# Seven products for the gate and up projections of two feed-forwards, with two weight sums made by accumulating transfers

## The chip, the cores and the metric

The kernel runs on one core of one Trainium2 chip. The metric is the device time of one execution in microseconds. TensorE multiplies, VectorE (DVE) and ScalarE (ACT) do the elementwise work, GpSimd (POOL) issues some transfers and clears a few tiles, and SyncE (SP) issues most transfers.

## The reference

One inference step of a two-layer decoder trunk, for a prompt of 512 tokens with 16 meta tokens and for 8 sample tokens (536 columns in all), width 1024, in float32. Each layer is a feed-forward, a mixer and a second feed-forward:

```python
def swiglu(h, w_gu, w_down):
    gate, up = jnp.split(h @ w_gu, 2, axis=-1)      # w_gu: 1024 x 5632
    return (jax.nn.silu(gate) * up) @ w_down         # w_down: 2816 x 1024
x += 0.5 * swiglu(rmsnorm(x, g), ...); x += mix(rmsnorm(x, g)); x += 0.5 * swiglu(rmsnorm(x, g), ...)
```

The mixer of layer 0 is convolution beside windowed attention; that of layer 1 is a state-space scan (SSM), whose output passes through a gated linear unit (GLU).

## The kernel before

Activations stand transposed: eight residual tiles `x[d]` of 128 rows (width) by 536 columns (tokens), in two halves of 268. float32 products are made from exact high and low parts: weights `whi`, `wlo` and activations `xh`, `xl`. `gemm` (L130) makes, for each 128-row slice `k` of the contraction and each half, three matmuls of 268 columns: `whi*xh`, `whi*xl`, `wlo*xh`. A 128x1024 weight block thus costs 8 x 3 x 2 = 48 matmuls.

`weights` (L117) loads such a block on SP's queue into `raw` (4 buffers), ACT rounds it to `whi` (L126, 3 buffers) and DVE subtracts to get `wlo` (L127, 3 buffers).

`ffn` (L255) goes in three chunks of 8, 8 and 6 hidden tiles. Of each hidden tile it makes a gate product and an up product (a pair of blocks, 96 matmuls), scales both by the norm's factor `R` (L273, L275), takes the silu (L274), multiplies (L276) and splits the result into `mh`, `ml` (`put`, L143, with ACT at L146 and DVE at L147). Then come the chunk's eight down products, added to the residual (L288). In the last chunk `finalize` (L149) scales and splits each finished residual tile into `xh`, `xl` (L155, L156) and sums its squares (L162, L163) for the next stage's norm, whose factor `rstd` (L179) computes.

`ssm_prep` (L758) is a generator of 45 steps that builds the matrices of layer 1's recurrence on DVE and stores them with 59 transfers on POOL's queue. It is advanced once per gate/up pair and once per down product (`filler`) through the second feed-forward of layer 0 and the first of layer 1, some 34 calls in each. `_mixer1` (L935) then runs the recurrence and ends with the GLU.

The program is written in one order; a scheduler orders each engine's queue ahead of the run by its own model of times and gives out buffers in turn. At run time each engine works its queue in order, waiting on semaphores. Accumulators are three pairs of PSUM banks (`mm` twice, `S` once, L95 to L103) and two single banks `ms`.

Of the kernel before, what the change touches and what calls it, by code (L numbers as in the profile page):

```python
# [26 lines left out]
NCK = 66            # chunks of 8 tokens in the prompt  # L27
# [3 lines left out]
LOENG = lambda nc: nc.vector  # L31
WHOLE, HEAD = 3, tuple((d,) for d in range(8))
# [28 lines left out]
class Trunk:  # L61
# [4 lines left out]
    # ---------------------------------------------------------------- pools  # L66
# [45 lines left out]
    # ------------------------------------------------------- building blocks  # L112
# [30 lines left out]
    def put(self, hi, lo, src):  # L143
        """src (fp32) -> exact high and low parts."""
# [4 lines left out]
    def finalize(self, d, g):  # L149
        """residual tile d is complete: its scaled split parts and its squares."""  # L150
# [3 lines left out]
        if g < 6:  # L154
# [99 lines left out]
    # ---------------------------------------------------------- feed-forward  # L254
    def ffn(self, wgu, wdn, gnext, filler=None, fin=None, head=None):  # L255
# [3 lines left out]
        for f0, nf in ((0, 8), (8, 8), (16, 6)):  # L259
            for i in range(nf):  # L260
# [20 lines left out]
            if f0 == 16 and fin is not None:  # L281
                self.down_last(fin, dn, nf)
                return
            for d in range(ND):
# [6 lines left out]
                if filler is not None and d < 6:  # L291
# [62 lines left out]
        # the samples' convolution up to the new row  # L354
# [19 lines left out]
        # states that are moved, not computed  # L374
# [7 lines left out]
    def mixer0(self, p, gnext):  # L382
# [12 lines left out]
        # gated conv input  # L395
# [3 lines left out]
        def z_tile(c):  # L399
# [7 lines left out]
            # sigmoid(g) = (1 + tanh(g / 2)) / 2: the table set that holds exp, too  # L407
# [19 lines left out]
        def conv_pe(i):  # L427
            """eight taps of the last tile's convolution, as products with diagonal matrices"""
# [18 lines left out]
        # keys, values, queries  # L447
# [858 lines left out]
```

## Time and profile before

| | |
|---|---|
| runs shown, us | 2070.46, 2066.05, 2066.57; median 2066.57 |
| span of the profiled execution | 2071.1 us (the page gives no other time of it) |
| busy: TensorE, DVE, ACT, POOL | 98%, 55%, 31%, 6% of the span |
| matmuls | 16302 |
| mean granted clock of TensorE | 0.989 of full speed |
| bytes moved by transfers | 213.51 MB, mean 103 GB/s |

Busy times are sums of the intervals in which an engine had an instruction running. A TensorE that is busy all the time may still be running its pipeline at its normal pace, so the distance between starts of matmuls is the measure of its work. The span is what the profiler saw between the first and the last instruction.

### The profile page before, as it was taken

The numbers are of one execution on the slowest core, as the hardware profiler recorded it, in microseconds if no ns is written. First come the engines' busy times: TensorE is split into PE (matmuls) and PEld (weight loads), VectorE is DVE, ScalarE is ACT, GpSimd is POOL, SyncE is SP. The second block draws the span as 40 slices with busy tenths as digits, with TensorE's granted clock in tenths as the row PEclk, the third lists the DMA queues.
The fourth block names the chain that finished last, engine by engine and source line by source line (L and its number), as shares of the span: only waits on it lengthen the run. The fifth ranks groups of instructions, "written<-read, shape, count | busy, mean of one in ns | idle before, by whom it ended". The sixth has DMA issues, their size and how long they took to land.

```text
span 2071.1 us, 37762 instructions
## 1 busy us (share of the span) xinstructions
PE 2023.6 (98%) x16302; PEld 1981.4 (96%) x16302; DVE 1133.5 (55%) x1819; ACT 644.8 (31%) x970; POOL 114.4 (6%) x172
## 2 busy tenths in 40 slices
PE   6999999999999999999999999999989999999998
PEld 5999999998779999999999999999989999999998
DVE  4443434479967874655575544345784444344336
ACT  3322222333446322322242222123324332122223
POOL 2000000012200000000010000000110000000000
PEclk9999999999979999999999999999999999999999
DMA  6432332232005343344344433623682323332321
GB/s 174 113 100 84 91 92 86 79 84 52 27 19 129 112 129 92 105 122 115 97 133 121 119 109 109 181 81 91 185 256 77 92 87 88 92 92 83 91 77 57
DMA packets 371494, 213.51 MB, mean 103 GB/s; under 512 B 36119, under 2 KB 362323, under 8 KB 370921
## 3 DMA queue, kind: packets, MB, share of 16 engines
q1 hardware_dynamic: 354897, 190.63, 32.1%
q0 software_dynamic: 5872, 19.40, 3.1%
q8 instruction: 128, 2.10, 0.4%
q10 hardware_dynamic: 10560, 1.09, 0.4%
q14 instruction: 37, 0.30, 0.0%
HBM read 193.14 MB, written 23.65 MB: 105 GB/s over the span
## 4 chain that ended last, share of the span: by engine, by line
PE 91%; DVE 5%; DMA 1%; ACT 1%; issue 1%; SPq 1%; ACTq 0%; DVEq 0%
PE mm L137 39%; PE mm L140 19%; PE S L137 18%; PE S L140 9%; DVE yc L425 1%; PE S L598 1%; DVE wlo L127 1%; DMA raw<-in_ffn_w_gu 1%; PE ms L606 0%; PE ms L887 0%; DMA mC<-dC 0%; PE ms L612 0%; DVE Sc L1029 0%; SPq L203 0%; PE ms L919 0%
## 5 line engine op out<-in xcount | busy, mean ns | idle before, releaser
L126 ACT ACTIVATE whi<-raw 128x1024 fp32r<-128x1024 f32 (+2 forms) x324 | 329.5, 1017 | 1138.9 <-PE mm L137 533.5
L137 PE MATMUL mm<-xh,whi 128*128 128x268 f32 x2144 | 445.2, 289 | 7.4 <-DVE tb L406 2.6
L137 PE MATMUL mm<-xl,whi 128*128 128x268 f32 x2144 | 442.1, 287 | 0.0
L140 PE MATMUL mm<-xh,wlo 128*128 128x268 f32 x2144 | 441.6, 287 | 0.0
L127 DVE TENSOR_TENSOR wlo<-raw,whi 128x1024 fp32r<-128x1024 f32 (+2 forms) x324 | 381.1, 1177 | 67.7 <-ACT whi L126 59.8
L137 PEld LDWEIGHTS mm<-xh,whi 128*128 128x128 f32 x2144 | 335.0, 189 | 10.2 <-DVE tb L406 3.0
L137 PEld LDWEIGHTS mm<-xl,whi 128*128 128x128 f32 x2144 | 336.2, 189 | 1.1 <-issue 0.5
L140 PEld LDWEIGHTS mm<-xh,wlo 128*128 128x128 f32 x2144 | 335.1, 188 | 2.0 <-issue 1.7
L137 PE MATMUL mm<-mh,whi 128*128 128x268 f32 x1216 | 258.6, 290 | 1.9 <-DVE xl L156 1.1
L140 PE MATMUL mm<-mh,wlo 128*128 128x268 f32 x1216 | 256.3, 287 | 0.8 <-DVE wlo L127 0.8
L137 PE MATMUL mm<-ml,whi 128*128 128x268 f32 x1216 | 256.4, 288 | 0.0
L137 PE MATMUL S<-xh,whi 128*128 128x268 f32 x1024 | 212.3, 288 | 2.6 <-DVE us L985 2.6
L137 PE MATMUL S<-xl,whi 128*128 128x268 f32 x1024 | 210.3, 287 | 0.0
L140 PE MATMUL S<-xh,wlo 128*128 128x268 f32 x1024 | 210.1, 287 | 0.0
L137 PEld LDWEIGHTS mm<-mh,whi 128*128 128x128 f32 x1216 | 193.2, 190 | 3.5 <-ACT whi L126 2.1
L140 PEld LDWEIGHTS mm<-mh,wlo 128*128 128x128 f32 x1216 | 192.9, 189 | 1.5 <-DVE wlo L127 1.0
L137 PEld LDWEIGHTS mm<-ml,whi 128*128 128x128 f32 x1216 | 193.7, 190 | 0.4 <-issue 0.2
L137 PEld LDWEIGHTS S<-xh,whi 128*128 128x128 f32 x1024 | 160.4, 189 | 3.1 <-issue 2.9
L137 PEld LDWEIGHTS S<-xl,whi 128*128 128x128 f32 x1024 | 160.6, 189 | 0.1
L140 PEld LDWEIGHTS S<-xh,wlo 128*128 128x128 f32 x1024 | 160.0, 189 | 0.0
L275 DVE TENSOR_TENSOR tb<-mm,R 128x536 f32<-128x536 f32 x60 | 43.0, 717 | 193.5 <-PE mm L140 193.1
L288 DVE SCALAR_TENSOR_TENSOR x<-mm,x 128x536 f32<-128x536 f32 x59 | 42.2, 716 | 163.1 <-PE mm L140 163.1
(455 smaller groups left out, 2203.3 us busy)
## 6 DMA issues: line engine op xcount, KB each, us to landing
raw<-in_ffn_w_gu SPq DMA_DIRECT2D x174, 512.0 KB
raw<-in_ffn_w_down SPq DMA_DIRECT2D x64, 512.0 KB
raw<-in_ffn_w_down SPq DMA_DIRECT2D x32, 384.0 KB
raw<-in_ssm_w_glu SPq DMA_DIRECT2D x16, 512.0 KB
raw<-in_ab_w_in SPq DMA_DIRECT2D x10, 512.0 KB
dC<-CL POOLq DMA_DIRECT2D x32, 128.0 KB, 3.0
dB<-B POOLq DMA_DIRECT2D x8, 512.0 KB, 3.5
dT<-dK POOLq DMA_DIRECT2D x8, 512.0 KB, 4.9
```

What stands on the lines that cost most here:

```text
L126: nc.scalar.activation(hi[:, :K], raw[:, :K], AF.Copy)
L127: nc.vector.tensor_sub(lo[:, :K], raw[:, :K], hi[:, :K].bitcast(F32))
L137: nc.tensor.matmul(ps[:, h, :HT], hi[:, k, :], src[:, h * HT:(h + 1) * HT], start=(k == 0 and i == 0), stop=False)
L140: nc.tensor.matmul(ps[:, h, :HT], lo[:, k, :], xh[k][:, h * HT:(h + 1) * HT], start=False, stop=(k == K - 1))
L275: nc.vector.tensor_mul(halves(b[:]), pu[:, :, :HT], R)
L288: nc.vector.scalar_tensor_tensor(x, ps[:, :, :HT], 0.5, x, op0=OP.mult, op1=OP.add)
L425: nc.vector.scalar_tensor_tensor(y, z, wcol(c, j), y, op0=OP.mult, op1=OP.add)
L598: nc.tensor.matmul(S[:, g, :w], qT[t][rw, 128 * b:128 * b + 128], kT[rw, k0:k0 + w], start=False, stop=True)
```

## The change

In both feed-forwards of layer 1 (`gnext` 3 leads into the first, 5 into the second), gate and up of one hidden tile are made together, by the form of Strassen's method with seven products and fifteen sums. The 2x2 blocks are: gate and up (rows), the two halves of the contraction (`k0`, `k1`), and the two halves of the tokens (`l`, `r`). Each product has 4 slices of `k` and one half of the columns, 4 x 3 = 12 matmuls; a pair has 7 x 12 = 84 in place of 96.

On the weight side, three sums are made per pair: `S` holds `u[k0]+u[k1]` in its second half and that plus `g[k0]` in its first, `U[k0]` becomes `u[k0]+g[k0]`, and `q = S[k0]+g[k1]`. The second half of `S` and the first of `U` are made by loading on SP and then adding with an accumulating transfer on POOL's queue (`DMASUM`); the other two are DVE additions. `sraw`, `sq4`, `qh` and `ql` have one buffer. On the activation side `operands` makes the four sums when a residual tile is finished.

The seven products stand in the order P1, P2, P4 of the pair before, P6, P3 of the pair before, P5, P7 (`SLOTS`); within a chunk alone. The SSM preparation is advanced twice per item, in the second feed-forward of layer 0 alone, and is finished ahead of the down products of its last chunk. The GLU is taken out of the mixer's tile pool, and the pool of the final norm is opened after the last pair.

```diff
+SLOTS = dict(P1=0, P2=1, P6=3, P5=5, P7=6, P4=9, P3=11)
+STRASSEN, DMASUM = (3, 5), True
     def finalize(self, d, g):
-        if g < 6:
+        if g in STRASSEN:
+            self.operands(d, col)
+        elif g < 6:
+    def operands(self, d, col):
+        nc, k = self.nc, d % 4
...
+        if d < 4:
...
+            w, b = self.t1[k], self.b12[k]
+            nc.scalar.activation(w[:, l], x[:, l], AF.Copy, scale=col)
+            nc.scalar.activation(b[:], x[:, r], AF.Copy, scale=col)
+            nc.vector.tensor_sub(w[:, r], w[:, l], b[:])
+            self.put(self.xh[d][:], self.xl[d][:], w[:])
+            return
+        w, b = self.t1[k], self.b12[k]
+        u, e, f = t("ou"), t("oe"), self.fx.tile([128, HT], F32, name="of")
+        nc.scalar.activation(u[:], x[:], AF.Copy, scale=col)
+        self.put(self.xh[d][:], self.xl[d][:], u[:])
+        nc.vector.scalar_tensor_tensor(e[:, l], w[:, r], -1.0, u[:, r], op0=OP.mult, op1=OP.subtract)
+        nc.vector.tensor_sub(e[:, r], u[:, r], b[:])
+        self.put(self.eh[k][:], self.el[k][:], e[:])
+        nc.vector.scalar_tensor_tensor(f[:], e[:, l], -1.0, u[:, l], op0=OP.mult, op1=OP.subtract)
+        self.put(self.fh[k][:], self.fl[k][:], f[:])
+    def seven_weights(self, gu, f):
...
+        G, gh, gl = self.wtiles()
+        U, uh, ul = self.wtiles()
+        S = self.fx.tile([128, 8, 128], F32, name="sraw")
+        sh, sl = (self.wts.tile([128, 8, 128], F32R, name=n, bufs=3) for n in ("whi", "wlo"))
...
+        nc.sync.dma_start(G[:], g)
+        if DMASUM:
+            nc.sync.dma_start(S[:, k1], u[:, k1])
+            nc.sync.dma_start(U[:], u)
+            nc.gpsimd.dma_start(S[:, k1], u[:, k0], accum_op=OP.add)
+            nc.gpsimd.dma_start(U[:, k0], g[:, k0], accum_op=OP.add)
...
+        split(gh, gl, G)
...
+        nc.vector.tensor_add(S[:, k0], S[:, k1], G[:, k0])
+        split(sh, sl, S)
+        nc.vector.tensor_add(q[:], S[:, k0], G[:, k1])
...
+        split(uh, ul, U)
+        split(qh, ql, q)
...
+        return {"P1": (gh, gl, 0, X(self.xh[:4], l), X(self.xl[:4], l)),
+                "P2": (gh, gl, 4, X(self.xh[4:], l), X(self.xl[4:], l)),
+                "P3": (qh, ql, 0, X(self.xh[4:], r), X(self.xl[4:], r)),
+                "P4": (uh, ul, 4, X(self.fh, l), X(self.fl, l)),
+                "P5": (sh, sl, 4, X(self.xh[:4], r), X(self.xl[:4], r)),
+                "P6": (sh, sl, 0, X(self.eh, l), X(self.el, l)),
+                "P7": (uh, ul, 0, X(self.eh, r), X(self.el, r))}
+    def seven(self, gu, f0, nf):
...
+            X, Y, Z = s["xy"][:, 0, :HT], s["xy"][:, 1, :HT], s["z"][:, :HT]
+            ps, first, last = {"P1": (X, 1, 0), "P2": (Z, 1, 1), "P6": (X, 0, 0), "P5": (Y, 1, 0), "P7": (X, 0, 0),
+                               "P4": (X, 0, 1), "P3": (Y, 0, 1)}[p]
...
+            if p == "P1":
+                nc.scalar.activation(sn[:, l], X, AF.Copy)
+                if f0 + n == 0:
+                    self.rstd()
+            elif p == "P2":
+                nc.vector.tensor_add(a[:, l], sn[:, l], Z)
+            elif p == "P6":
+                nc.scalar.activation(sn[:, r], X, AF.Copy)
+            elif p == "P7":
+                nc.scalar.activation(u3[:], X, AF.Copy)
+                nc.vector.tensor_add(b[:, r], u3[:], Y)
+            elif p == "P4":
+                nc.scalar.activation(b[:, l], X, AF.Copy)
+            elif p == "P3":
+                nc.vector.tensor_add(a[:, r], sn[:, r], Y)
+                nc.vector.tensor_mul(a[:], a[:], self.R[:])
+                nc.scalar.activation(a[:], a[:], AF.Silu)
+                nc.vector.tensor_mul(a[:], a[:], self.R[:])
+                nc.vector.scalar_tensor_tensor(b[:], b[:], -1.0, a[:], op0=OP.mult, op1=OP.mult)
+                self.put(self.mh[n][:], self.ml[n][:], b[:])
     def ffn(self, wgu, wdn, gnext, filler=None, fin=None, head=None, seven=None, then=None):
...
+            if seven:
+                self.seven(gu, f0, nf)
+            for i in range(0 if seven else nf):
...
                     next(filler, None)
+                    next(filler, None)
...
+            if f0 == 16:
+                if seven:
+                    seven.close()
+                if then:
+                    then()
...
     def run(self, ctx):
...
+        def then():
+            self.finish(prep)
+            sp.close()
+            self.extra(fx.enter_context(tc.tile_pool(name="fx", bufs=1)))
+        self.ffn(io["ffn2_w_gu"][0], io["ffn2_w_down"][0], 3, prep, then=then)
+        self.ffn(io["ffn1_w_gu"][1], io["ffn1_w_down"][1], 4, seven=fx)
+        fx = ExitStack()
+        self.mixer1(5, lambda: self.extra(fx.enter_context(tc.tile_pool(name="fx", bufs=1))))
+        self.ffn(io["ffn2_w_gu"][1], io["ffn2_w_down"][1], None, fin=True, seven=fx)
```

## Rows read from the trace of the kernel before

**Rows 1.** The page's first part: busy us (share of the span) and instructions.

```profile
PE 2023.6 (98%) x16302; PEld 1981.4 (96%) x16302; DVE 1133.5 (55%) x1819; ACT 644.8 (31%) x970; POOL 114.4 (6%) x172
```

**Rows 2.** Stretches of three feed-forwards: us, each engine's busy us, clock, DMA share, GB/s.

```profile
657.00:1058.00 401.00, 401.00 (x3285) 399.31 (x3284) 253.63 (x489) 118.14 (x153) 24.28 (x45) 1.00 0.39 114
1058.00:1460.00 402.00, 402.00 (x3289) 400.13 (x3289) 196.42 (x254) 116.39 (x147) 17.99 (x35) 1.00 0.40 116
...
1660.00:2071.10 411.10, 402.92 (x3260) 402.00 (x3258) 181.04 (x275) 113.82 (x155) 2.98 (x3) 0.99 0.29 84
```

**Rows 3.** TensorE's timeline in the last feed-forward: start, us, instruction (24 rows per block).

```profile
1704.22 0.42 PE L137 MATMUL mm<-xh,whi 128*128 128x268 f32 x2
...
1710.16 0.42 PE L137 MATMUL mm<-xh,whi 128*128 128x268 f32 x2
```

**Rows 4.** SP queue's waits, whole span: us in total, times, longest.

```profile
SPq L125 <- DVE wlo L127: 1555.2, 283, 42.6
```

**Rows 5.** TensorE's timeline of a product of one half, twelve rows.

```profile
2043.20 0.29 PE L137 MATMUL mm<-mh,whi 128*128 128x268 f32 x1
...
2044.56 0.29 PE L140 MATMUL mm<-mh,wlo 128*128 128x268 f32 x1
```

**Rows 6.** Groups by line and form: count, busy us, mean ns, idle before.

```profile
L127 DVE TENSOR_TENSOR wlo<-raw,whi 128x1024 fp32r<-128x1024 f32 x276 | 339.6, 1231 | 67.0 <-ACT whi L126 59.2
...
L126 ACT ACTIVATE whi<-raw 128x1024 fp32r<-128x1024 f32 x276 | 292.5, 1060 | 1044.0 <-PE mm L137 493.0 <-issue 312.1 <-PE S L137 238.9
...
L276 DVE TENSOR_TENSOR tb<-tb,ta 128x536 f32<-128x536 f32 x88 | 63.0, 716 | 9.3 <-ACT ta L274 2.9
...
L127 DVE TENSOR_TENSOR wlo<-raw,whi 128x512 fp32r<-128x512 f32 x16 | 10.8, 681 | 0.6 <-ACT whi L126 0.5
...
L126 ACT ACTIVATE whi<-raw 128x512 fp32r<-128x512 f32 x16 | 10.0, 624 | 10.9 <-PE mm L140 5.0 <-PE mm L137 4.9 <-DMA craw<-in_ssm_c_re 1.0
...
L172 ACT ACTIVATE ta<-ms,eps 128x268 f32<-128x268 f32 x14 | 6.2, 481 | 1.5 <-PE ms L185 1.4
...
L175 DVE SCALAR_TENSOR_TENSOR tb<-ms,tb 128x268 f32<-128x268 f32 x14 | 5.6, 431 | 0.1
```

**Rows 7.** Timeline of DVE between two pairs of the last feed-forward.

```profile
1746.00 0.72 DVE L275 TENSOR_TENSOR tb<-mm,R 128x536 f32<-128x536 f32 x1 [3.82 <-PE mm L140]
...
1746.83 0.72 DVE L276 TENSOR_TENSOR tb<-tb,ta 128x536 f32<-128x536 f32 x1
...
1747.46 1.22 DVE L127 TENSOR_TENSOR wlo<-raw,whi 128x1024 fp32r<-128x1024 f32 x1
...
1748.60 0.71 DVE L147 TENSOR_TENSOR ml<-tb,mh 128x536 fp32r<-128x536 f32 x1
```

**Rows 8.** SP's timeline: the issue of one 512 KB weight load.

```profile
1701.19 0.37 SPq L125 DMA_DIRECT2D raw<-in_ffn_w_gu  x1
```

**Rows 9.** Share of the DMA engines, 1701.1 to 1706.5 us in 40 slices of 0.135.

```profile
DMA  0000000015699999999995210000000000000000
```

**Rows 10.** DMA issues: count, KB each, median us from issue to landing.

```profile
dT<-dK POOLq DMA_DIRECT2D x8, 512.0 KB, 4.9
...
pT<-in_cache_win_k POOLq DMA_DIRECT2D x2, 256.0 KB, 3.5
...
pT<-in_state_conv POOLq DMA_DIRECT2D x2, 240.0 KB, 8.0
```

**Rows 11.** Timeline where the second of these feed-forwards begins: the last residual tile.

```profile
1060.22 0.72 DVE L288 SCALAR_TENSOR_TENSOR x<-S,x 128x536 f32<-128x536 f32 x1 [0.64 <-PE S L140]
...
1060.97 0.74 ACT L155 ACTIVATE xh<-x,gcols 128x536 fp32r<-128x536 f32 x1
...
1062.61 0.77 DVE L156 SCALAR_TENSOR_TENSOR xl<-x,gcols,xh 128x536 fp32r<-128x536 f32 x1
```

**Rows 12.** Stretches in the state-space mixer, columns as in the second group.

```profile
1505.00:1509.50 4.50, 1.89 (x34) 1.69 (x31) 4.45 (x10) 1.03 (x2) 0.32 (x1) 1.00 0.95 279
1509.50:1513.00 3.50, 3.50 (x18) 3.50 (x17) 3.44 (x7) 0.65 (x1) 1.24 (x1) 0.51 0.94 327
```

More of the change, by code (lines that the diff above doesn't have):

```diff
@@ L163, in finalize, with extra @@
             nc.vector.tensor_add(self.sq[:], self.sq[:], s[:])
+    def extra(self, pool):
+        self.fx = pool
+        t = lambda n, w: pool.tile([128, w], F32R, name=n)
+        self.eh, self.el = ([t(f"{n}{k}", NT) for k in range(4)] for n in ("eh", "el"))
+        self.fh, self.fl = ([t(f"{n}{k}", HT) for k in range(4)] for n in ("fh", "fl"))
+    def operands(self, d, col):
+        nc, k = self.nc, d % 4
+        x, l, r = self.x[d], slice(0, HT), slice(HT, NT)
+        t = lambda n, bufs=1: self.fx.tile([128, NT], F32, name=n, bufs=bufs)
+        if d < 4:
+            if d == 0:
+                self.b12 = [self.fx.tile([128, HT], F32, name=f"b12{i}") for i in range(4)]
+                self.t1 = [self.fx.tile([128, NT], F32, name=f"t1{i}") for i in range(4)]
+            w, b = self.t1[k], self.b12[k]
[13 more added lines that the diff above has]
+        self.put(self.fh[k][:], self.fl[k][:], f[:])
@@ new lines, in seven_weights, with split @@
+    def seven_weights(self, gu, f):
+        nc = self.nc
+        k0, k1 = slice(0, 4), slice(4, 8)
+        G, gh, gl = self.wtiles()
+        U, uh, ul = self.wtiles()
+        S = self.fx.tile([128, 8, 128], F32, name="sraw")
+        sh, sl = (self.wts.tile([128, 8, 128], F32R, name=n, bufs=3) for n in ("whi", "wlo"))
+        q = self.fx.tile([128, 4, 128], F32, name="sq4")
+        qh, ql = (self.fx.tile([128, 4, 128], F32R, name=n) for n in ("qh", "ql"))
+        g, u = gu[:, :, f:f + 128], gu[:, :, D_FF + f:D_FF + f + 128]
+        nc.sync.dma_start(G[:], g)
[4 more added lines that the diff above has]
+            nc.gpsimd.dma_start(U[:, k0], g[:, k0], accum_op=OP.add)
+        else:
+            nc.sync.dma_start(U[:], u)
+        def split(h, l, r):
+            nc.scalar.activation(h[:], r[:], AF.Copy)
+            nc.vector.tensor_sub(l[:], r[:], h[:].bitcast(F32))
+        split(gh, gl, G)
+        if not DMASUM:
+            nc.vector.tensor_add(S[:, k1], U[:, k0], U[:, k1])
+        nc.vector.tensor_add(S[:, k0], S[:, k1], G[:, k0])
+        split(sh, sl, S)
+        nc.vector.tensor_add(q[:], S[:, k0], G[:, k1])
+        if not DMASUM:
+            nc.vector.tensor_add(U[:, k0], U[:, k0], G[:, k0])
+        split(uh, ul, U)
+        split(qh, ql, q)
+        l, r = slice(0, HT), slice(HT, NT)
+        X = lambda t, c: [a[:, c] for a in t]
+        x0, x1 = slice(0, 4), slice(4, 8)
+        return {"P1": (gh, gl, 0, X(self.xh[:4], l), X(self.xl[:4], l)),
[5 more added lines that the diff above has]
+                "P7": (uh, ul, 0, X(self.eh, r), X(self.el, r))}
@@ new lines, in seven @@
+    def seven(self, gu, f0, nf):
+        nc = self.nc
+        l, r = slice(0, HT), slice(HT, NT)
+        st, zs = {}, None
+        for n, p in sorted(((n, p) for n in range(nf) for p in SLOTS), key=lambda a: 7 * a[0] + SLOTS[a[1]]):
+            if p == "P1":
+                if n % 2 == 0:
+                    zs = self.scores()
+                w = self.seven_weights(gu, (f0 + n) * 128)
+                st[n] = dict(w=w, xy=self.acc2(), z=zs[:, n % 2], sn=self.fx.tile([128, NT], F32, name="sn", bufs=2),
+                             u3=self.fx.tile([128, HT], F32, name="u3"), a=self.work("ta"), b=self.work("tb"))
+            s = st[n]
+            X, Y, Z = s["xy"][:, 0, :HT], s["xy"][:, 1, :HT], s["z"][:, :HT]
+            ps, first, last = {"P1": (X, 1, 0), "P2": (Z, 1, 1), "P6": (X, 0, 0), "P5": (Y, 1, 0), "P7": (X, 0, 0),
+                               "P4": (X, 0, 1), "P3": (Y, 0, 1)}[p]
+            hi, lo, c, bh, bl = s["w"][p]
+            for k in range(4):
+                for i, (w, b) in enumerate(((hi, bh), (hi, bl), (lo, bh))):
+                    nc.tensor.matmul(ps, w[:, c + k, :], b[k], start=bool(first and k + i == 0),
+                                     stop=bool(last and k == 3 and i == 2), skip_group_check=True)
+            sn, u3, a, b = s["sn"], s["u3"], s["a"], s["b"]
+            if p == "P1":
+                nc.scalar.activation(sn[:, l], X, AF.Copy)
[17 more added lines that the diff above has]
+                self.put(self.mh[n][:], self.ml[n][:], b[:])
+                del st[n]
@@ L279, in ffn @@
                     next(filler, None)
+                    next(filler, None)
             dn = wdn[f0 * 128:(f0 + nf) * 128].rearrange("(k p) f -> p k f", p=128)
-            if f0 == 16 and fin is not None:
-                self.down_last(fin, dn, nf)
-                return
+            if f0 == 16:
[3 more added lines that the diff above has]
+                    then()
+                if fin:
+                    with tc.tile_pool(name="fin", bufs=1) as p:
+                        self.down_last(p, dn, nf)
+                    return
             for d in range(ND):
@@ L290, in ffn @@
                     self.finalize(d, gnext)
-                if filler is not None and d < 6:
+                if filler is not None and d < 6 and f0 < 16:
+                    next(filler, None)
                     next(filler, None)
```

22 lines of the change are left out of this document (10 added, 12 removed).

## The prediction

> **What bounds the kernel now.** I read the busy shares first: TensorE is busy 98% of the span, DVE 55%, ACT 31% [rows 1]. Then the stages: in the feed-forwards TensorE has no idle time at full clock (401 of 401 us, 402 of 402) while DVE works half of it [rows 2]; the reader should see that only fewer or shorter matmuls can shorten these stretches. Then the pace: two weight blocks begin at 1704.22 and 1710.16, 48 matmuls in 5.94 us, so 123.75 ns each [rows 3]; the columns of 280 to 290 ns that a matmul shows are pipelined and mean nothing here. Last the supply: SP waited 1555 us in all for DVE to free a `raw` buffer [rows 4], so weights are early and no transfer is late. The change therefore buys matmuls with DVE work, transfers and new waits; the question is what becomes late next.
>
> **Products.** 44 pairs (22 in each of two feed-forwards) lose 96 - 84 = 12 matmuls: 528 x 0.12375 = 65.3 us. A pair goes from 11.88 to 10.40 us. A product now writes one half's bank twelve times in a row instead of alternating; the pace of that is in the trace: twelve matmuls from 2043.20 to 2044.56, eleven steps of 0.1236 us [rows 5]. So the pace stays.
>
> **DVE and ACT per pair.** Before, DVE has two `wlo` of 1.23 us and four operations of 0.72: 5.3 us. After: three `wlo` of 1.23 and one of half size (0.68), two weight sums of half size (0.68, taken as the half-size subtraction), three half-width sums from PSUM (0.43), four full-width operations (0.72): 3.69 + 0.68 + 1.36 + 1.29 + 2.88 = 9.9 us [rows 6]. Operations that don't depend on each other overlap by 0.08 to 0.09: that of 1.22 us at 1747.46 is followed at 1748.60; a dependent one starts 0.11 after its predecessor's end [rows 7]. Thirteen operations thus take 8.8 us (all overlapping) to 11.3 us (none). I take 8.8, since the scheduler puts other work between dependent ones: 85% of 10.40. ACT: 3 x 1.06 + 0.62 for the rounding, four half-width copies at 0.48 and two full-width operations under 0.75, 7.2 us: 69%. Both fit beside TensorE, at no cost; if DVE doesn't, that is the second rival.
>
> **The loop of the one `sraw` buffer.** This is the wait that the change adds. The next pair's load into `S` may begin only when the last reader of this pair's `S` is done; then come, one after the other: the load of 256 KB, the accumulating transfer, the DVE sum, the rounding on ACT, the subtraction on DVE. SP issued a load of 512 KB at 1701.19 [rows 8]; its packets ran in slices 8 to 24, from 1.0 to 3.2 us after the issue [rows 9], so half of it takes 1.0 + 1.1 = 2.1 us. No accumulating transfer is in this trace. The nearest row is the POOL transfer of 256 KB from DRAM into SBUF, 3.5 us to landing; 512 KB on the same queue among weight loads took 4.9, and 240 KB in a burst at the start 8.0 [rows 10]. Its destination has to be read too, by between nothing and another 1.1 us (256 KB more at the load's rate); I take 0.5. So the loop is 2.1 + 3.5 + 0.5 + 0.68 + 1.06 + 1.23 = 9.1 us with nothing in the way. To that I add half an operation in progress at each of the three engine steps (0.35 x 0.85 twice, 0.35 x 0.69), 0.85 us, and the sharing of the DMA engines: the pair's two 512 KB loads hold them for 4.3 of 10.4 us, 41%, and the two pieces of 1.05 us each meet one that often: 0.85 us. Together 10.8, against 10.40 that TensorE needs: 0.4 us late per pair. The first pair of a chunk has its `S` ready (2.3 us of ACT and DVE work before P6, which begins after P1 and P2, 2.97 us), so 7 + 7 + 5 = 19 pairs per feed-forward pay, 38 in all: 15.2 us. Bounds: 9.1 us (nothing lost, gain whole) and 15 us (8.0 us landing).
> Behind the waiting DVE sum stand the subtractions of `S`, `U` and `q` and the sums that read the product banks; behind the waiting rounding on ACT, the bank copies; on SP the load of `U` and the next `G`; on POOL the addition into `U`. All are waited for by TensorE only later, so one lateness is paid once per pair, not twice.
> The page DMA: Bandwidth & Descriptors of the Trainium skill, section on the anatomy of a GpSimd-issued DMA, fits 2.0 us + bytes / 436e3, an estimate of 2.6 us for 256 KB where the row has 3.5. By that the loop would fit and the 15.2 us would go.
>
> **Ends of chunks.** The last pair of a chunk has nobody behind it: P4 follows P7 in the same bank and must wait for ACT's copy, 0.48 us and a handover, say 0.6. After P3 come a half sum, four full-width operations, the rounding and handovers, some 4.7 us, while the down product's first 7 slices (42 matmuls) give 5.2 us of cover, 3.7 us with 6 tiles. Per feed-forward 3 x 0.6 + 1.0: 6 us in all (0 to 10).
>
> **Starts of the two feed-forwards.** Before, the chain after the last residual tile is short and covered: the addition at 1060.22, rounding 1060.97, subtraction 1062.61 [rows 11], while the first product needs this tile only after 42 matmuls. Now P1 (1.49 us) needs tiles 0 to 3 alone, but P2 needs tile 7, which is scaled, then rounded, then subtracted: 0.72 + 0.74 + 0.74 (taken as the scaling) + 0.72 and handovers, 3.1 us; 1.6 us idle. P6 needs `eh`, two half sums and a split more, 2.3 us behind P2's 1.49: 0.8. In the first of the two, DVE also falls behind: tiles 4 to 7 cost it 5.5 us each (addition 0.72, next weights 0.95, between half and full size, two half and one more half sum, three splits, squares) against 36 matmuls, 4.46 us; four times 1.0 less overlaps, I take 2.5. Idle time of this length has lowered the clock in this trace: 1505 to 1509.5 has 1.9 us of TensorE work, and the next 3.5 us ran at 0.51 [rows 12], worth 1.7 us. Sum 4.9 + 2.4 + 2 x 1.7 = 10.7 us (2 to 14). Of TensorE's two levels, 1.2 and 2.4 GHz, that is the lower.
>
> **SSM preparation.** Its DVE work is what the two stretches of layers 0 and 1 have over the plain one: 253.6 + 196.4 - 2 x 181.0 = 88 us [rows 2]. After, nearly all of it stands beside one feed-forward: 253.6 + 15.4 + some 12 us of new operand sums = 281 of 401 us. Two steps of 2 us, 1.23 and 0.72 make 6 us per down product of 5.94; the weights split ahead cover that. Cost nothing; without cover up to 5 us. Its 45 steps are spent by the 56 calls before the last chunk's end, and its 59 POOL transfers are past before the first accumulating one stands on that queue; SP's queue is not touched by it, and its loads stand on ACT's, where they were.
> The closing and opening of pools moves no work: the final norm's tiles are first written after the first down product, which waits for the last pair anyway. Nothing.
>
> **Sum.** -65.3 + 15.2 + 6 + 10.7 = -33.4 us. The profiled span is 2071.1 us; the median of the runs shown is 2066.6, 4.5 lower; I take the difference off the median: 2033.
>
> **Rivals.**
> All hidden: the loop stays under 10.4 us. For it: the loads are steady and SP's waits long [rows 4]; against: four handovers and 85% DVE. -65.3 + 16.7 = -48.6: 2018. Chance 0.27.
> DVE is the bound: if its operations don't overlap, a pair takes 11.3 us, 44 x (11.3 - 11.88) = -25.5, + 16.7 = -8.8: 2058. For it: sums feed on each other; against: what overlaps in rows 7. Chance 0.12.
> Slower: the accumulating transfer. Everything else leaves 48.6 us of gain over 38 pairs, 1.28 us each, so from a loop of 11.7 us on, that is a landing of 4.9 us in all in place of 4.0, the kernel is slower. With 4.9 for the transfer and its own re-reading of 0.5 on top, the loop is 12.2, 38 x 1.8 = 68, and the kernel 20 slower, 2086. For it: 4.9 and 8.0 in rows 10, both with other traffic; against: they moved twice the bytes or were queued behind others. Chance 0.20.
> The same page of the Trainium skill, section on issuing engines not being separate DMA queues, says that transfers of all queues interleave on the same 16 DMA engines, which speaks for this rival; rows 10 show nothing at the load of the new pairs.
> That the products are not fewer is excluded by the listing: 84 calls per pair.
>
> **Numbers.** Forecast as summed 0.34 (its own range 2024 to 2048), all hidden 0.27, DVE 0.12, the slow loop 0.20, and 0.07 for costs that just meet the gain. 0.2% (4 us) is about what a measurement of this kernel can tell. Faster 0.34 + 0.27 + 0.12 = 0.73, same 0.07, slower 0.20. The range runs from 2008 (all hidden and half of the 16.7 too) to 2084, leaving out one in ten at either end.
>
> **What would show it.** Matmuls 16302 - 528 = 15774. In the windows of pairs: starts of P1 10.4 to 10.8 us apart; idle TensorE ahead of P6, put down to `sl` or to `sh`; behind that a DVE sum on `S` that waited for a POOL transfer landing about 4.0 us after issue. DVE at 80 to 85% there. A gap of 2 to 5 us at each start of the two feed-forwards with a stretch of clock near half after it. Wrong if pairs take over 11.7 us, if DVE is busy without a pause, or if the gaps stand before P1, which would be the weight buffers.

## The result, and the profile after

The changed kernel takes 2132.61 us (median of four runs, 2130.80 to 2136.59) against 2068.52 for the kernel before: ratio 1.0305, 95% interval 1.0285 to 1.0324. It is 64 us slower where 33 us less were forecast, and it lies above the range. The profiled execution took 2132.69 us, with a span of 2130.9.

The page's first part answers to [rows 1].

```profile
PE 2006.3 (94%) x15774; PEld 1946.5 (91%) x15774; DVE 1327.5 (62%) x2175; ACT 789.1 (37%) x1274; POOL 226.6 (11%) x260
```

The 528 matmuls are gone (16302 to 15774), and yet TensorE's share fell from 98% to 94% of a longer span: the matmuls are saved, and TensorE stands idle for longer than that saves. The next view has the three stretches of pairs in the first of the two feed-forwards (8, 8 and 6 pairs), the columns as in [rows 2].

```profile
1063.20:1171.00 107.80, 92.90 (x661) 89.62 (x660) 74.05 (x113) 54.10 (x86) 17.79 (x14) 0.91 0.59 125
1221.10:1325.00 103.90, 88.97 (x654) 86.57 (x654) 65.99 (x93) 46.88 (x75) 17.76 (x14) 0.93 0.61 132
1375.80:1450.00 74.20, 64.50 (x488) 63.25 (x487) 48.17 (x68) 33.15 (x53) 11.58 (x9) 0.95 0.58 123
```

The reader should see three things. The 22 pairs take 285.9 us, 13.0 each, where 10.40 were the matmuls' own and 11.88 the price before: 57 us too much in this feed-forward; the same three stretches of the other take 279.9 us, 51 too much. DVE works 64 to 69% of the time, so it is not full. And the clock is no longer 1.00 as in [rows 2]: 0.91 to 0.95, part of the time at the lower of TensorE's two levels (1.2 GHz of 2.4).

The mean granted clock fell from 0.989 over 2071.1 us to 0.972 over 2130.9, by its own measure 22.8 and 59.7 us lost: up to 37 more, since it counts idle stretches too. The distances between matmul starts that are over 0.3 us, each less a matmul's 0.124, sum to 54.8 us before and 146.6 after: 92 more. The distances of 0.18 to 0.3 us, among which matmuls at the lower level stand, make 38.7 and 72.7 by the same count: 34 more. With -65.3 for the matmuls that is +61, against +59.8 between the spans; the account closes to 1 us.

What ended TensorE's idle time ahead of the products (line L268, matmuls alone, us in total and times); three of these groups of matmuls, with that idle time at the end of the row; and what DVE's sum on `S` (L231) waited for:

```profile
  DVE wlo L227: 27.9, 10
  ACT sn L272: 16.1, 7
  DVE ta L286: 8.2, 5
  DVE tb L281: 6.1, 4
  ACT whi L226: 4.8, 6
```

```profile
L268 PE MATMUL S<-xh,wlo 128*128 128x268 f32 x176 | 53.7, 305 | 22.6 <-DVE wlo L227 22.6
L268 PE MATMUL mm<-eh,whi 128*128 128x268 f32 x352 | 106.4, 302 | 20.3 <-ACT sn L272 16.1 <-ACT whi L226 3.6 <-issue 0.5
L268 PE MATMUL mm<-eh,wlo 128*128 128x268 f32 x352 | 105.3, 299 | 5.4 <-DVE wlo L227 5.4
```

```profile
  DMA sraw<-in_ffn_w_gu: 114.0, 37
```

Of 73 us in all, TensorE waits only 9.0 for parts of the sum `S` itself: 5.4 and 3.6 ahead of P6, which multiplies it by `eh`. The 22.6 us stand ahead of P2, the one product that goes into the bank `S` (a PSUM bank, not the sum), and are for the low part of `G`; the rest are copies and sums of product banks (`sn`, `ta`, `tb`). DVE's sum waits 114 us for a transfer into `sraw`, in 37 of 44 pairs, and `G`'s subtraction stands behind it in DVE's queue, here with its rounding done since 1099.39:

```profile
1104.66 0.69 DVE L231 TENSOR_TENSOR sraw<-sraw,raw 128x512 f32<-128x512 f32 x1 [5.80 <-DMA sraw<-in_ffn_w_gu]
1105.27 1.22 DVE L227 TENSOR_TENSOR wlo<-raw,whi 128x1024 fp32r<-128x1024 f32 x1
```

P2 went on at 1106.54, at the subtraction's end. One turn of the loop in the timeline (start, us, engine, operation):

```profile
1894.81 0.69 DVE L231 TENSOR_TENSOR sraw<-sraw,raw 128x512 f32<-128x512 f32 x1 [1.55 <-DMA sraw<-in_ffn_w_gu]
1895.54 0.69 DVE L233 TENSOR_TENSOR sq<-sraw,raw 128x512 f32<-128x512 f32 x1
1896.14 0.71 DVE L289 TENSOR_TENSOR ta<-ta,R 128x536 f32<-128x536 f32 x1
1896.89 0.72 DVE L290 SCALAR_TENSOR_TENSOR tb<-tb,ta 128x536 f32<-128x536 f32 x1
1897.52 1.22 DVE L227 TENSOR_TENSOR wlo<-sraw,whi 128x1024 fp32r<-128x1024 f32 x1
1898.77 0.37 SPq L219 DMA_DIRECT2D sraw<-in_ffn_w_gu  x1
1902.86 1.30 POOL L221 DMA_DIRECT2D sraw<-in_ffn_w_gu  x1 [8.14 <-DMA sraw<-in_ffn_w_gu]
1907.68 0.69 DVE L231 TENSOR_TENSOR sraw<-sraw,raw 128x512 f32<-128x512 f32 x1 [0.78 <-DMA sraw<-in_ffn_w_gu]
```

From sum to sum 12.9 us. SP issues the next load 0.03 us after the last reader's end (1897.52 + 1.22); then 4.09 us pass until POOL adds, and 4.82 until DVE sums. Pairs of over 11.7 us were named ahead as what would make the prediction wrong. The transfers' own table:

```profile
sraw<-in_ffn_w_gu SPq DMA_DIRECT2D x44, 256.0 KB
sraw<-in_ffn_w_gu POOLq DMA_DIRECT2D x44, 256.0 KB, 5.0
raw<-in_ffn_w_gu POOLq DMA_DIRECT2D x44, 256.0 KB, 4.7
```

Over the 38 pairs that don't begin a chunk, taken from the starts of these instructions, the loop has a mean of 14.30 us (median 13.95), against 10.8 in the forecast. Its stages, with the forecast's half operations and its sharing put where they belong (means, us):

| stage | forecast | measured | difference |
|---|---|---|---|
| last reader's end to POOL's start (the load) | 2.1 + 0.43 = 2.53 | 4.05 | 1.52 |
| POOL's start to DVE's sum (the adding transfer) | 4.0 + 0.43 + 0.30 = 4.73 | 5.11 | 0.38 |
| sum to rounding | 0.68 + 0.24 = 0.92 | 1.49 | 0.57 |
| rounding to subtraction | 1.06 + 0.30 = 1.36 | 1.46 | 0.10 |
| subtraction to the last reader's end | 1.23 | 2.19 | 0.96 |

The load is mis-sized most. A quiet one shows why: SP issues it at 1687.03, POOL, which waits for it alone by then, starts adding at 1690.39, and nothing else moves in between. The two instructions, and under them the share of the DMA engines from 1686.9 to 1690.9 us in 40 slices of 0.1 us:

```profile
1687.03 0.37 SPq L219 DMA_DIRECT2D sraw<-in_ffn_w_gu  x1
1690.39 1.28 POOL L221 DMA_DIRECT2D sraw<-in_ffn_w_gu  x1 [9.47 <-DMA sraw<-in_ffn_w_gu]
...
DMA  0000000000013387678998642100000000000000
```

Packets run from 1.0 to 2.5 us after the issue, and another 0.9 us passes before the waiting engine starts. The forecast ended the load with its last packet, and gave the packets 1.1 us where they take 1.5. The page DMA: Bandwidth & Descriptors of the Trainium skill, section on the anatomy of a GpSimd-issued DMA, says for that path that the semaphore moves only when the last byte's receipt is in; the 0.9 us here, on SP's path, agree in kind. The last row of the table has another cause: in 16 of the 38 pairs (every second one from a chunk's fourth on) the reader that ends last is the sum `q` (L233), which stands in DVE's queue behind sums of the pair before and ends 3.0 to 4.0 us after the subtraction's start instead of 1.23. The third row's difference lies in six pairs: in the second pair of each chunk the rounding starts 3.0 to 9.3 us after the sum, in the 32 others 0.8.

### The profile page after: what moved, and what is told of

The parts are those of the page before. It is cut to its first block, busy times and chain, and to the rows that moved or that the text cites. A ratio compares the mean times of both kernels' runs of the same rounds, so it can differ in the third digit from the quotient of the medians.

```text
span 2130.9 us, 37928 instructions
## 1 busy us (share of the span) xinstructions
PE 2006.3 (94%) x15774; PEld 1946.5 (91%) x15774; DVE 1327.5 (62%) x2175; ACT 789.1 (37%) x1274; POOL 226.6 (11%) x260
## 4 chain that ended last, share of the span: by engine, by line
PE 72%; DMA 11%; DVE 10%; issue 3%; ACT 3%; SPq 1%; ACTq 0%; DVEq 0%; POOLq 0%
PE mm L139 27%; PE mm L142 13%; PE S L139 12%; DMA sraw<-in_ffn_w_gu 10%; PE mm L268 8%; PE S L142 6%; DVE wlo L227 2%; DVE yc L566 1%; ACT whi L226 1%; PE S L268 1%; PE S L739 1%; DVE wlo L129 1%; DMA raw<-in_ffn_w_gu 1%; DVE ta L289 1%; DVE tb L290 1%
## 5 line engine op out<-in xcount | busy, mean ns | idle before, releaser
L129 DVE TENSOR_TENSOR wlo<-raw,whi 128x1024 fp32r<-128x1024 f32 (+2 forms) x236 | 272.8, 1158 | 64.0 <-ACT whi L128 59.5
L139 PE MATMUL mm<-xl,whi 128*128 128x268 f32 x1280 | 266.3, 289 | 0.0
L142 PE MATMUL mm<-xh,wlo 128*128 128x268 f32 x1280 | 265.7, 288 | 0.0
L139 PEld LDWEIGHTS mm<-xh,whi 128*128 128x128 f32 x1280 | 201.2, 190 | 11.0 <-issue 3.6
L142 PEld LDWEIGHTS mm<-xh,wlo 128*128 128x128 f32 x1280 | 201.6, 190 | 2.0 <-issue 1.7
L139 PEld LDWEIGHTS mm<-xl,whi 128*128 128x128 f32 x1280 | 202.2, 190 | 1.1 <-issue 0.5
L227 DVE TENSOR_TENSOR wlo<-raw,whi 128x1024 fp32r<-128x1024 f32 x88 | 107.5, 1222 | 47.1 <-ACT whi L226 46.2
L139 PE MATMUL S<-mh,whi 128*128 128x268 f32 x604 | 128.1, 289 | 0.6 <-ACT whi L128 0.6
L139 PE MATMUL S<-ml,whi 128*128 128x268 f32 x604 | 127.6, 287 | 0.0
L142 PE MATMUL S<-mh,wlo 128*128 128x268 f32 x604 | 127.2, 286 | 0.0
L268 PE MATMUL mm<-eh,whi 128*128 128x268 f32 x352 | 106.4, 302 | 20.3 <-ACT sn L272 16.1
L268 PE MATMUL mm<-xh,whi 128*128 128x268 f32 x352 | 103.4, 296 | 11.5 <-DVE ta L286 8.2
L231 DVE TENSOR_TENSOR sraw<-sraw,raw 128x512 f32<-128x512 f32 x44 | 30.5, 692 | 129.1 <-DMA sraw<-in_ffn_w_gu 114.0
```

What stands on the lines that cost most here:

```text
L129: nc.vector.tensor_sub(lo[:, :K], raw[:, :K], hi[:, :K].bitcast(F32))
L139: nc.tensor.matmul(ps[:, h, :HT], hi[:, k, :], src[:, h * HT:(h + 1) * HT], start=(k == 0 and i == 0), stop=False)
L142: nc.tensor.matmul(ps[:, h, :HT], lo[:, k, :], xh[k][:, h * HT:(h + 1) * HT], start=False, stop=(k == K - 1))
L227: nc.vector.tensor_sub(l[:], r[:], h[:].bitcast(F32))
L231: nc.vector.tensor_add(S[:, k0], S[:, k1], G[:, k0])
L268: nc.tensor.matmul(ps, w[:, c + k, :], b[k], start=bool(first and k + i == 0), stop=bool(last and k == 3 and i == 2), skip_group_check=True)
```

## The experiments

Theory: the loop through `sraw` costs the 100 us between forecast and result, and the work that stands behind it in the engines' queues makes it worse. Rivals: accumulating transfers cost by themselves (engines, POOL, bandwidth); DVE or the starts of the feed-forwards are what is late; the preparation that was moved. Ratios are to the kernel before, in runs made beside them (medians 2069.72, 2071.12 and 2069.34 us for the three sets).

**All four sums on DVE** (e1_dvesum). No transfer adds, and `sraw` is filled by DVE.

```diff
-STRASSEN, DMASUM = (3, 5), True
+STRASSEN, DMASUM = (3, 5), False
```

> All four weight sums on DVE, no accumulating transfers. Theory (the loop of the one sraw buffer, 14.0 us per pair as measured, 8.9 of it two transfers): the loop shrinks to about 4.5 us, pairs are held by TensorE (10.4 us) or by DVE (8.2 us busy per pair now, 9.6 then); most of the 114 us that the six chunks of pairs take above 10.4 us per pair goes: 2030 to 2060 us. Rival (the loss lies at the starts of the two feed-forwards, the lowered clock and the order of the queues, not in the transfers): less than 30 us gained, 2100 or more. Rival (DVE is the bound): DVE busy above 95% in the chunks and 2080 or more.

Measured: 2032.74 us, ratio 0.9823 (0.9800 to 0.9847). Stretches of its pairs:

```profile
1090.00:1150.00 60.00, 59.52 (x477) 59.01 (x476) 55.87 (x84) 35.19 (x56) 0.00 (x0) 1.00 0.33 98
1250.00:1310.00 60.00, 60.00 (x484) 59.70 (x483) 45.39 (x67) 27.96 (x45) 0.00 (x0) 1.00 0.33 97
```

Without the two transfers the seven products gain what they should: 484 matmuls in 60.00 us, 0.124 each, at full clock. DVE is busy 93% of the first stretch, more than in any of the three above, and TensorE loses 0.5 us of 60 there. So the loss is made by the accumulating sums and not by the products, and DVE is no bound: this also ends the rival of the prediction by which DVE's operations don't overlap.

**Two buffers for `sraw`** (e2_sraw2).

```diff
-        S = self.fx.tile([128, 8, 128], F32, name="sraw")
+        S = self.fx.tile([128, 8, 128], F32, name="sraw", bufs=2)
```

> Two sraw buffers in place of one, all else as changed. Theory (one buffer): the loop of 14.0 us may take two pairs, 7.0 us each, so it no longer decides: 2030 to 2060 us, at the same bytes and transfers. Rival (the transfers share the DMA engines and are late as such): the transfers are as many and as long, 2100 or more.

Measured: 2147.93 us, ratio 1.0376 (1.0352 to 1.0399): slower still, where 2030 to 2060 were expected. The bare form of the theory, one buffer too few, falls with it. Its DVE timeline shows why:

```profile
1908.87 0.69 DVE L231 TENSOR_TENSOR sraw<-sraw,raw 128x512 f32<-128x512 f32 x1 [2.98 <-DMA sraw<-in_ffn_w_gu]
1909.48 0.71 DVE L289 TENSOR_TENSOR ta<-ta,R 128x536 f32<-128x536 f32 x1
1910.23 0.72 DVE L290 SCALAR_TENSOR_TENSOR tb<-tb,ta 128x536 f32<-128x536 f32 x1
1910.86 1.22 DVE L227 TENSOR_TENSOR wlo<-sraw,whi 128x1024 fp32r<-128x1024 f32 x1
```

In the order of the built program, the sum L231 here is that of the next pair, and the subtraction behind it belongs to this pair. With a second buffer free, the scheduler put the next pair's sum ahead of this pair's subtraction, in all 38 pairs that have a next one in their chunk; its model of times may have had the transfer landed by then, which no run here shows. On the chip it had not, DVE stands 2.98 us, and the subtraction that would release the buffer for the load after that stands behind. Two buffers then turn more slowly than one: from the third pair of each chunk on (26 distances), sum to sum takes 15.0 us in the mean, against 13.9 in the changed kernel. This gives the theory its second form: the order of DVE's queue closes the loop.

**The adding transfer into a tile that nobody reads** (e3_nowait).

```diff
+        self.junk = pool.tile([128, 4, 128], F32, name="junk")
+        self.nc.gpsimd.memset(self.junk[:], 0.0)
...
-            nc.gpsimd.dma_start(S[:, k1], u[:, k0], accum_op=OP.add)
+            nc.gpsimd.dma_start(self.junk[:], u[:, k0], accum_op=OP.add)
```

> The accumulating transfer into S goes into a tile that nobody reads, so one weight sum is left out of the result; bytes, queues and transfers are as in the changed kernel. Theory (loop): 14.0 - 5.1 = 8.9 us, under 10.4, so pairs are held by TensorE again: 2030 to 2065 us. Rival (contention of the transfers): unchanged within 20 us of 2132.

Measured: 2126.2 us in one run, far from the theory's 2065 and within the rival's 20 us of 2132. But it decides little, since the edit made a new wait. POOL's timeline at the start of the first of the two feed-forwards:

```profile
1065.80 1.28 POOL L223 DMA_DIRECT2D junk<-in_ffn_w_gu  x1 [3.46 <-DMA junk<-in_ffn_w_gu]
1070.71 1.28 POOL L223 DMA_DIRECT2D junk<-in_ffn_w_gu  x1 [3.63 <-DMA junk<-in_ffn_w_gu]
1075.79 1.29 POOL L223 DMA_DIRECT2D junk<-in_ffn_w_gu  x1 [3.80 <-DMA junk<-in_ffn_w_gu]
1080.76 1.28 POOL L223 DMA_DIRECT2D junk<-in_ffn_w_gu  x1 [3.68 <-DMA junk<-in_ffn_w_gu]
1081.51 1.85 POOL L224 DMA_DIRECT2D raw<-in_ffn_w_gu  x1
```

Each addition into the one tile waits for the last, 5 us apart, and the addition into `U`, which TensorE needs, stands behind a row of them on POOL: 27 us without a matmul at the start of either feed-forward, and half clock after. The four chunks that don't begin a feed-forward take 354 us from the first matmul of their pairs to the last, against 393 in the changed kernel: a part of the loss goes there, not the whole. It is the same mistake once more, on another queue: work that waits for a transfer ahead of work that doesn't.

**The move of the SSM preparation alone** (e4_prep): the kernel before with that part of the diff.

```diff
-            self.ffn(io["ffn2_w_gu"][0], io["ffn2_w_down"][0], 3, prep)
-            self.ffn(io["ffn1_w_gu"][1], io["ffn1_w_down"][1], 4, prep)
-            self.finish(prep)
+            self.ffn(io["ffn2_w_gu"][0], io["ffn2_w_down"][0], 3, prep, then=lambda: self.finish(prep))
+        self.ffn(io["ffn1_w_gu"][1], io["ffn1_w_down"][1], 4)
```

> The kernel before with the SSM preparation alone moved: two steps per item in the second feed-forward of layer 0, the rest ahead of its last down products. Theory: nothing, 2064 to 2073 us, since the stretch from the second feed-forward of layer 0 on differs by some 4 us between the traces. Rival (the crowded preparation is part of the loss): 2080 or more.

Measured: 2069.89 us, ratio 1.0000 (0.9989 to 1.0012). The move costs nothing; that step stands.

**One adding transfer at a time** (e5_usum, e6_ssum). In the first, DVE makes `S[k1]` and a transfer adds into `U`; in the second the other way round.

```diff
# e5_usum
-            nc.sync.dma_start(S[:, k1], u[:, k1])
-            nc.gpsimd.dma_start(S[:, k1], u[:, k0], accum_op=OP.add)
+            nc.vector.tensor_add(S[:, k1], U[:, k0], U[:, k1])
# e6_ssum
-            nc.gpsimd.dma_start(U[:, k0], g[:, k0], accum_op=OP.add)
+        nc.vector.tensor_add(U[:, k0], U[:, k0], G[:, k0])
```

> Only U's sum stays with an accumulating transfer (into raw, four buffers); the sum for S's second half goes to DVE, so that sraw is filled by no transfer. Theory A (the loss is the chain of load, accumulating transfer and DVE sum through sraw, with DVE's queue standing behind it): the loss goes almost whole, 2030 to 2045 us, gaps of TensorE inside the chunks under 1 us each. Theory B (accumulating transfers cost by themselves, each takes DMA engines, POOL or DVE's time whichever tile they go to): half of the 100 us between the two ways of summing stays, about 2080 us.

> The other half: S's second half by the accumulating transfer as in the changed kernel, U's sum on DVE. Theory A: the loop of sraw is untouched, 13.5 to 14.5 us for a pair, 2115 to 2145 us. Theory B: one of the two accumulating transfers less, about 2080 us. With a shorter landing of the accumulating transfer into sraw (4 us or less in place of 5.0), because it no longer shares with U's, the loop would be 1 us shorter, about 2095 us.

Measured: 2037.54 us, ratio 0.9845 (0.9819 to 0.9870), and 2128.37, ratio 1.0273 (1.0252 to 1.0294). The addition into `U`, whose tile has four buffers, costs some 5 us against DVE's, which the intervals leave open; the one into `sraw` keeps 96 of the 100 us. Theory B, an accumulating transfer's own price wherever it goes, falls. With `U`'s transfer gone, the landing of the one into `sraw` is 4.8 us in place of 5.0: the two hardly share.

**Halves apart: order and buffers** (e7_halves, e9_half1, e11_free). The half that is loaded and added to becomes a tile `S1` of its own, DVE's sum goes into another, `S0`, and the split of `S` is made in two pieces, in all three runs.

```diff
-        S = self.fx.tile([128, 8, 128], F32, name="sraw")
+        S0 = self.fx.tile([128, 4, 128], F32, name="sum0")
+        S1 = self.fx.tile([128, 4, 128], F32, name="sraw", bufs=2)
...
-        nc.vector.tensor_add(S[:, k0], S[:, k1], G[:, k0])
-        split(sh, sl, S)
+        nc.vector.tensor_add(S0[:], S1[:], G[:, k0])
+        split(sh[:, k0], sl[:, k0], S0)
+        split(sh[:, k1], sl[:, k1], S1)
# e9_half1, on top
-        S1 = self.fx.tile([128, 4, 128], F32, name="sraw", bufs=2)
+        S1 = self.fx.tile([128, 4, 128], F32, name="sraw", bufs=1)
# e11_free, on top of e7_halves
-        S0 = self.fx.tile([128, 4, 128], F32, name="sum0")
+        S0 = self.fx.tile([128, 4, 128], F32, name="sum0", bufs=2)
```

> Both accumulating transfers stay, but the half that is loaded and accumulated has two buffers of its own and DVE's sum goes into a third tile with one buffer, so the sum of the next pair can't stand ahead of this pair's subtraction in DVE's queue; the split of S is cut in two halves (some 0.3 us more of DVE and ACT for each pair). Theory A in its form 'DVE's queue order closes the loop even with two buffers': the load may run a whole pair ahead, 9 us of transfers in 20.8 us, and the time falls to 2035 to 2060 us. Rival (the transfers cannot keep up, whatever the order): 2110 us or more, as with two whole buffers (2148).

> As e7_halves, but with one buffer for the loaded and accumulated half in place of two; the DVE sum's own tile stays. If the loop through one buffer is what costs, the order being right: the load waits for the subtraction of the pair before, 3.9 (load) + 5.1 (accumulate) + 0.7 (sum) + two half roundings and a half subtraction (about 2 us with handovers) = 11.7 to 13 us a pair against 10.4, 38 x 1.3 to 2.6 = 50 to 100 us above e7_halves: 2075 to 2125 us. Rival (the order alone costs, one buffer is enough once the sum has its own tile): 2026 to 2040 us.

> As e7_halves, but with two buffers for the DVE sum's tile, so that in DVE's queue the next pair's sum stands ahead of this pair's subtractions again, as the listing of the built program shows. Theory (the order of DVE's queue turns two buffers into one): the loop is 3.9 + 5.1 + 0.7 + the three or four operations behind the sum, about 12 us, and the time 2085 to 2145 us. Rival (e7_halves is fast because the two halves are released apart, or because sraw has two buffers): 2024 to 2035 us.

Measured, with the buffers of `S1` and `S0`:

| | `S1` | `S0` | us | ratio, interval |
|---|---|---|---|---|
| e7_halves | 2 | 1 | 2026.51 | 0.9787 (0.9770 to 0.9804) |
| e9_half1 | 1 | 1 | 2137.56 | 1.0327 (1.0307 to 1.0347) |
| e11_free | 2 | 2 | 2102.73 | 1.0168 (1.0146 to 1.0190) |

With both adding transfers in it, e7_halves is 106 us faster than the changed kernel, and faster than the 2035 to 2060 us expected of it. It and e11_free do the same work; e11_free has one buffer more, and is 76 us slower. DVE's queue in e11_free, and then in e7_halves:

```profile
1883.61 0.69 DVE L232 TENSOR_TENSOR sum<-sraw,raw 128x512 f32<-128x512 f32 x1 [3.72 <-DMA sraw<-in_ffn_w_gu]
...
1886.40 0.68 DVE L228 TENSOR_TENSOR wlo<-sum,whi 128x512 fp32r<-128x512 f32 x1
1887.00 0.68 DVE L228 TENSOR_TENSOR wlo<-sraw,whi 128x512 fp32r<-128x512 f32 x1
...
1896.84 0.69 DVE L232 TENSOR_TENSOR sum<-sraw,raw 128x512 f32<-128x512 f32 x1 [4.09 <-DMA sraw<-in_ffn_w_gu]
```

```profile
1912.95 0.69 DVE L228 TENSOR_TENSOR wlo<-sum,whi 128x512 fp32r<-128x512 f32 x1 [2.12 <-ACT whi L227]
1913.56 0.69 DVE L228 TENSOR_TENSOR wlo<-sraw,whi 128x512 fp32r<-128x512 f32 x1
1914.16 0.69 DVE L232 TENSOR_TENSOR sum<-sraw,raw 128x512 f32<-128x512 f32 x1
```

In e11_free the next pair's sum stands ahead of this pair's subtraction in all 38 pairs, in e7_halves in none. With one tile for the sum, it can't be queued before this pair's subtraction has read the old one; it starts at once when its turn comes, its transfer having landed before. Sum to sum takes 11.1 us there and 13.9 in e11_free, counted as above. Over the whole run it waited for `sraw`'s transfers not once in e7_halves, and 103.4 us in 31 pairs in e11_free. What TensorE's matmuls waited for in e11_free is telling too:

```profile
  DVE tb L283: 36.2, 16
  DVE ta L288: 14.8, 11
```

Not weights, but the sums that read its product banks, queued behind the waiting sum. The page PSUM — Partial Sum Buffer of the Trainium skill, section on engine and sequencer instructions, calls the DVE queue strictly first in, first out; the two traces agree. The 76 us are the price of the order that came with the buffer: the scheduler placed some entries of the queues of ACT, SP and TensorE otherwise too, and that the sum's place is what costs is read from these waits.

e9_half1 was expected between 2075 and 2125 us and came out above. The order of its sum is forced as in e7_halves, but the one buffer's load starts only when the subtraction is done, and that stands behind other work in every second pair: the sum at 1893.20 is followed by the subtraction at 1898.69 and the next sum at 1908.41. So, with the split in two pieces throughout, both are needed, two buffers for what the transfers fill and an order in which nothing that waits stands ahead of a release.

**Writing in place of adding** (e10_plain).

```diff
-            nc.gpsimd.dma_start(S[:, k1], u[:, k0], accum_op=OP.add)
+            nc.gpsimd.dma_start(S[:, k1], u[:, k0])
```

One of the two terms of `S[k1]` is left out of the result by this.

> The changed kernel with the POOL transfer into sraw writing in place of adding (the second half of S then lacks one of its two terms). If the landing falls from 5.0 us to the 3.5 us of the plain POOL transfers of the kernel before, the loop falls from 14.0 to 12.5 us and the time by 38 x 1.5 = 57 us, to about 2075 us. If adding is not what makes it slow (POOL's own issue of 1.3 us and the shared engines are), the landing stays at 4.7 to 5.1 us and the time at 2120 to 2140 us.

Measured: 2093.73 us, ratio 1.0112 (1.0082 to 1.0143), between the two expectations. The same row of the transfers' table:

```profile
sraw<-in_ffn_w_gu POOLq DMA_DIRECT2D x44, 256.0 KB, 3.9
```

Adding costs 1.1 us over writing (5.0 to 3.9), of which POOL's issuing instruction, with 1.28 us in place of 0.78, can be 0.5. The median loop falls by the same 1.1, from 13.95 to 12.85, and the kernel by 39 us, 1.0 for each of the 38 pairs. Even a transfer that only writes leaves it slower than before.

**The starts** (e8_start, e12_best). In the first pair of a feed-forward P5, which needs only tiles 0 to 3, goes ahead of P2, and the norm's factor is made behind P7. Once with all sums on DVE, once with e7_halves.

```diff
-key=lambda a: 7 * a[0] + SLOTS[a[1]]):
+key=lambda a: .5 if a == (0, "P5") and not f0 else 7 * a[0] + SLOTS[a[1]]):
...
             if p == "P1":
                 nc.scalar.activation(sn[:, l], X, AF.Copy)
-                if f0 + n == 0:
-                    self.rstd()
...
                 nc.vector.tensor_add(b[:, r], u3[:], Y)
+                if f0 + n == 0:
+                    self.rstd()
```

> All sums on DVE, and at the start of each of the two feed-forwards P5 of the first pair, which needs tiles 0 to 3 alone, goes ahead of P2, and the norm's product and table load are moved behind P7. If the idle time of 8 us and the stretch at half clock at the start (idle 1068.6 to 1075.7) come from P2 and P6 waiting for the last tiles' operands with the norm in between: 2023 to 2029 us. If the operands on DVE and ACT are what ends last, whatever TensorE does meanwhile: 2031 to 2035 us, as without it.

> e7_halves with the start of e8_start (P5 of the first pair ahead of P2, the norm behind P7). e8_start gained 4 us over the DVE sums alone; if both gains add: 2019 to 2025 us, ratio 0.975 to 0.978. If they overlap: 2025 to 2028 us.

Measured: 2028.80 us, ratio 0.9793 (0.9774 to 0.9811), 4 us under e1_dvesum; and 2020.85, ratio 0.9771 (0.9750 to 0.9792), 6 us under e7_halves. In either comparison the intervals overlap, so the gain is likely and not settled. e12_best is the fastest of all: 48 us faster than the kernel before and 112 faster than the changed one. Its first part of the page:

```profile
PE 1965.1 (97%) x15774; PEld 1915.2 (95%) x15774; DVE 1335.5 (66%) x2219; ACT 798.4 (40%) x1318; POOL 227.0 (11%) x260
```

TensorE is busy 97% of the span, against 94% in the changed kernel.

## Why the prediction was wrong

**Products: right.** The matmuls went as listed, at 0.124 us each (e1_dvesum). In e12_best they are worth what was worked out, less a rest of 12.8 us by the spans (2018.6 and 2071.1: -52.5 = -65.3 + 12.8) or 16.8 by the medians (-48.5).

**DVE and ACT beside TensorE: right.** DVE at 64 to 69% in the changed kernel, up to 93% in e1_dvesum, at full pace of TensorE in both e1_dvesum and e7_halves.

**The loop of the one `sraw` buffer: this step failed.** The mechanism was named, a DVE sum that waits for a POOL transfer, but the loop was summed to 10.8 us and takes 14.3. By terms: the load 1.5 us short, since it ended with the last packet, with no time until the waiting engine starts; the last reader 1.0 short, since `q` and not the subtraction is last in 16 of the 38 pairs; the sum to the rounding 0.6 short, all of it in the second pair of each chunk. The term that looked most doubtful, the accumulating transfer, was short by 0.4 only.
The rule from loop to time was off as well, the other way: 38 x (14.3 - 10.4) = 148 us would give 2166. A chunk's first loop starts early: the load of the second pair at 1687.03 is issued 3.6 us before the chunk's first product, at 1690.67. Counted on TensorE, as time over 0.12375 us for each matmul, the pairs behind a chunk's first lose 100 us in all, 2.6 each; the forecast had 15.2.

**"All are waited for by TensorE only later": wrong.** That was said of what stands behind the waiting sum, and the idle time was looked for ahead of P6. In the changed kernel all but 9.0 of the 73 us ahead of the products are waits for other things, 22.6 of them for a subtraction behind the waiting sum; e11_free shows TensorE waiting 51 us for sums behind the waiting one, because banks come free late. The order of the queue was taken as harmless, where with two buffers it closes the loop. That a lateness is paid more than once per pair isn't shown: 2.6 us are lost where the loop is 3.9 over.

**The clock: priced at the starts alone.** The forecast has two stretches at half clock, 3.4 us. Gaps of 1 to 5 us in the pairs are followed by many more; by the distances above the slower matmuls took 34 us more in all than before. The gap at 1102.8 and what comes after it, in windows of the changed kernel:

```profile
1102.80:1106.60 3.80, 0.35 (x4) 0.14 (x2) 1.83 (x2) 1.08 (x2) 1.04 (x1) 0.85 1.01 125
1107.60:1111.00 3.40, 3.40 (x17) 3.40 (x17) 3.33 (x7) 0.65 (x1) 0.00 (x0) 0.50 0.00 0
```

17 matmuls in 3.4 us, where 27 fit at the full level: behind a gap of 3.7 us (no matmul starts from 1102.81 to 1106.54) this stretch alone loses 10 matmuls, another 1.2 us. What full clock would have saved is not shown: where the loop sets the pace, slower matmuls fill time in which TensorE would have waited. Some of it counts, for the chain that ended last also runs through products (start, us, what):

```profile
1899.91 7.72 PE mm L268 x48
```

These 48 matmuls stand behind a gap of 2.7 us, with a mean clock of 0.78, and take 5.94 us at the full level.

**Ends and starts, 16.7 us: the starts right, the sum in part by luck.** e7_halves, whose pairs run at nearly full pace, has -45.9 between the spans, that is 19.4 us for them and for all else (20.7 by the medians). By the count above, the first 60 matmuls of pairs in its two feed-forwards lose 11.1 us together (10.7 forecast), but the ends of its six chunks 1.1 in place of 6, and short gaps within the pairs, which were forecast at nothing, some 8. In the changed kernel the starts lose 16 and the ends 4.

**The preparation: right**, by e4_prep. The diff also advances the preparation of layer 0's mixer twice per item, which the prediction passed over; it did no harm, the factor of the norm ahead of layer 0's second feed-forward being written by 669.9 us against 673.8 before.

**The rivals.** The slow loop had the right mechanism and nearly the right landing (4.9 us and 0.5 for re-reading, measured 5.0), and its threshold held: loops of 14.3 us, and of 13.3 in the mean in e10_plain, make the kernel slower. Its time, 2086, was too low because its loop of 12.2 us had the load and the last reader of the forecast. It should have been the forecast: 4.9 was in the rows for a transfer beside other traffic, and the quiet row was taken. The fit on the page of the Trainium skill that the prediction weighed, an estimate of 2.6 us for 256 KB, is further off than the row of 3.5: 3.9 us was measured for writing and 5.0 for adding. "All hidden", 2018, is what the change gives when the loop is opened: 2020.85 in e12_best.

## What to carry to other kernels

A load ends for its consumer when the consumer starts: take the time from issue to the waiter's first instruction, not to the last packet, and add up a one-buffer loop from last reader to last reader, with the queue that the last reader stands in. Where an engine works in order, look for the instruction that waits longest and ask what stands behind it: a second buffer can make a kernel slower, if it lets a waiting instruction be queued ahead of the one that releases. An addition by transfer cost next to nothing here where its tile has buffers to spare (`U`) and what reads it is not queued before its time; in a loop of one buffer, load and addition took 9.2 us where DVE's own sum takes 0.69.

## What the runs showed that was not expected

An accumulating transfer of 256 KB from DRAM into SBUF lands 5.0 us after its issue, a writing one 3.9, and the issue alone holds POOL 1.28 us in place of 0.78. A quiet load on SP whose packets run 1.5 us took 3.4 us until its waiter started. One buffer more for a tile of 256 KB made the kernel 76 us slower. With DVE busy 93% of a stretch of 60 us, TensorE still worked 59.5.
